# Binary cross entropy on one core: who negates, and in how many pieces

## The chip, the cores and the metric

The kernel runs on one core of one Trainium2 chip. A core has five engines that run side by side, each with its own list of instructions: TensorE (PE, not used here), VectorE (DVE), ScalarE (ACT), GpSimd (POOL) and SyncE (SP). Sixteen DMA engines move data between the large memory (HBM) and the core's on-chip memory of 128 partitions (SBUF). A transfer is issued by an instruction on POOL, ACT or SP, goes into that engine's queue, and the DMA engines work the queue off in order. The metric is device time in microseconds (us); less is better. The time before is 1867.55 us, the median of 3 runs (1865.96 to 1867.95).

## The reference

Two float32 arrays of 8192 x 8192, `pred` and `target` (zeros and ones), give one of the same shape:

```python
eps = 1e-7
pred = np.clip(pred, eps, 1 - eps)
return -(target * np.log(pred) + (1 - target) * np.log(1 - pred))
```

Because a target is 0 or 1, the kernel computes the same as -log(|(target - 1) + pred|) after the clip: for target 1 this is -log(pred), for target 0 it is -log(1 - pred).

## The kernel before

**Tiles.** The arrays are seen as one flat row of elements, which is cut into 39 chunks. A chunk of width w is 128 partitions by w columns. Chunk 0 has 8192 columns, chunks 1 to 35 have `WIDE` = 14336, and the last three (`TAIL`) have 6656, 6656 and 1024. In the code `z` is 35, the last wide chunk, and `a, b, c` are the three tail chunks.

**Buffers.** `ring_p` holds three slots of 14336 float32 columns. A chunk's pred values are loaded into its slot, worked on in place by all steps, and stored from there. Chunk k + 2 uses the slot of chunk k - 1, so its load has to wait for that chunk's store. `ring_t` has room for one chunk of targets, which the load casts from float32 to bfloat16, so the targets of chunk k + 1 can be loaded only when chunk k has been merged.

**Steps of a chunk**, each on all columns or on one half of them (`halves`):
- `clip` (VectorE, L85): max with 1e-7, then min with 1 - 1e-7, one instruction.
- `merge` (L91, L94, L95): VectorE forms (target - 1) + pred; ScalarE then takes the absolute value (Abs), and then the logarithm (Ln).
- `negate` (VectorE, L99): times -1.
- `load_p` (L70), `load_t` (L73), `store` (L79): transfers. All are issued on POOL, but for the first pred load (ACT's queue) and the stores of the three tail chunks (SP's queue).

**Order.** The order on each engine is written out by hand (`manual_schedule`): an engine runs its instructions as they stand in the source, and waits at each for the data it needs. One turn of the loop over chunks (L110 to L120) gives, for chunk k: both halves merged; the targets of k + 1 loaded; both halves negated; both halves of chunk k + 1 clipped; chunk k stored; the pred values of k + 2 loaded. On VectorE a turn is therefore merge, merge, negate, negate, clip, clip; on ScalarE Abs, Ln, Abs, Ln; on POOL the issue of a target load, of a store, and of a pred load. A store waits for the second negation of its chunk, and the issues behind it on POOL wait with it. VectorE's clips stand behind the second negation, which waits for ScalarE's second Ln.

Of the kernel before, what the change touches and what calls it, by code (L numbers as in the profile page):

```python
# [1 line left out]

# [4 lines left out]

EPS = 1e-7

WIDE = 14336  # L10
SLOTS = 3
TAIL = (6656, 6656, 1024)
ROWS = (108, 12, 8)


@with_exitstack
def kernel(
    ctx: ExitStack,
    tc: tile.TileContext,
    pred: bass.AP,  # L20
    target: bass.AP,
    out: bass.AP,
):
    nc = tc.nc
    fp32 = mybir.dt.float32
    low = mybir.dt.bfloat16
    Alu = mybir.AluOpType
    Act = mybir.ActivationFunctionType
    P = nc.NUM_PARTITIONS

    R, C = pred.shape
    total = R * C // P
    rest = total - sum(TAIL)
    n = rest // WIDE
    first = rest - n * WIDE
    assert 0 < first <= WIDE and n > 4 and sum(TAIL) <= WIDE
    spots = [(first, 0)]
    spots += [(WIDE, k % SLOTS * WIDE) for k in range(1, n + 1)]
    c = (n + 1) % SLOTS * WIDE
    for w in TAIL:  # L40
        spots.append((w, c))
        c += w
    n = len(spots)
    z = n - 1 - len(TAIL)
    starts = [sum(w for w, _ in spots[:k]) * P for k in range(n)]

    pool = ctx.enter_context(tc.tile_pool(name="rings", bufs=1))
    ring_p = pool.tile([P, SLOTS * WIDE], fp32, name="ring_p", tag="ring_p")
    ring_t = pool.tile([P, WIDE], low, name="ring_t", tag="ring_t")
    warm = pool.tile([1, 8], fp32, name="warm", tag="warm")  # L50

    def chunk(ap, k):
        flat = ap.rearrange("r c -> (r c)")
        w = spots[k][0]
        return flat[starts[k] : starts[k] + w * P].rearrange("(p w) -> p w", p=P)

    def cols(ring, k, part, c):
        w = spots[k][0]
        i, m = part
        return ring[:, c + i * w // m : c + (i + 1) * w // m]  # L60

    def p_of(k, part=(0, 1)):
        return cols(ring_p, k, part, spots[k][1])

    def t_of(k, part=(0, 1)):
        return cols(ring_t, k, part, spots[k][1] % WIDE)

    def load_p(k):
        queue = nc.scalar if k == 0 else nc.gpsimd
        queue.dma_start(out=p_of(k), in_=chunk(pred, k))  # L70

    def load_t(k):
        nc.gpsimd.dma_start(out=t_of(k), in_=chunk(target, k))  # L73

    def store(k):
        queue = nc.sync if k > z else nc.gpsimd
        r = 0
        for rows in ROWS if k == n - 1 else (P,):
            queue.dma_start(out=chunk(out, k)[r : r + rows, :], in_=p_of(k)[r : r + rows, :])  # L79
            r += rows  # L80
        assert r == P

    def clip(k, *part):
        p = p_of(k, *part)
        nc.vector.tensor_scalar(  # L85
            out=p, in0=p, scalar1=EPS, scalar2=1 - EPS, op0=Alu.max, op1=Alu.min
        )

    def merge(k, *part):
        p, t = p_of(k, *part), t_of(k, *part)  # L90
        nc.vector.scalar_tensor_tensor(  # L91
            out=p, in0=t, scalar=1.0, in1=p, op0=Alu.subtract, op1=Alu.add
        )
        nc.scalar.activation(out=p, in_=p, func=Act.Abs)  # L94
        nc.scalar.activation(out=p, in_=p, func=Act.Ln)  # L95

    def negate(k, *part):
        p = p_of(k, *part)
        nc.vector.tensor_scalar(out=p, in0=p, scalar1=-1.0, scalar2=None, op0=Alu.mult)  # L99

    halves = (0, 2), (1, 2)
    with tc.manual_schedule():
        load_p(0)
        load_t(0)
        load_p(1)
        nc.vector.memset(warm, 1.0)  # L106
        nc.scalar.activation(out=warm, in_=warm, func=Act.Ln)  # L107
        for h in halves:
            clip(0, h)
        for k in range(z):  # L110
            for h in halves:
                merge(k, h)
            load_t(k + 1)
            for h in halves:
                negate(k, h)
            for h in halves:
                clip(k + 1, h)
            store(k)
            if k + 2 <= z:
                load_p(k + 2)  # L120
        for h in halves:
            merge(z, h)
        a, b, c = range(z + 1, n)
        for j in a, b, c:
            load_p(j)
            load_t(j)
        negate(z, halves[0])
        clip(a)
        negate(z, halves[1])
        store(z)  # L130
        merge(a)
        clip(b)
        merge(b)
        negate(a)
        store(a)
        clip(c)
        merge(c)
        negate(b)
        store(b)
        negate(c)  # L140
        store(c)


# [1 line left out]
_INS = ['pred', 'target']  # L145
_OUTS = [((8192, 8192), 'float32')]


# [23 lines left out]
```

## Time and profile before

| what | value |
|---|---|
| median of 3 runs | 1867.55 us |
| profiled execution | 1868.84 us, span 1867.1 us |
| VectorE busy | 1118.2 us, 60% of the span |
| ScalarE busy | 901.7 us, 48% |
| POOL busy | 283.3 us, 15% |
| moved by DMA (as written to SBUF or HBM) | 671.14 MB, mean 359 GB/s |
| HBM read, written | 536.87 MB, 268.44 MB |
| L91, merge on VectorE, 7168 columns | 70 times, mean 7.62 us |
| L94 Abs and L95 Ln on ScalarE, 7168 columns | 70 times each, mean 6.17 and 6.18 us |
| L85 clip and L99 negation on VectorE, 7168 columns | 70 times each, mean 3.89 us |

How to read the profile. Times in it are us from the start of the span unless marked ns. A row of the timeline gives start, duration, engine, line of the source, operation, the buffer written and read, the shape, and how many like instructions in a row were merged into it (x2); in square brackets stands how long the engine sat idle before it and whose end it waited for. An issue on POOL is shown as DMA_DIRECT2D with the time that POOL spends on it. A slice row gives the span in 40 equal parts, the busy share of each as a digit in tenths (9 is 90% or more). The chain that ended last is followed back from the last instruction, at each step to what released it; "issue" is time in it for which the profile shows no wait. A window row gives, for a stretch of the span, the busy time of each engine with the number of instructions, the share of the DMA engines' time that was busy, and the GB/s moved; bytes and busy time of a DMA packet are booked where the packet starts, so in windows of 1 us or less shares over 1 and zeros alternate.

### The profile page before, as it was taken

The numbers are of one execution on the slowest core, as the hardware profiler recorded it, in microseconds if no ns is written. First come the engines' busy times: TensorE is split into PE (matmuls) and PEld (weight loads), VectorE is DVE, ScalarE is ACT, GpSimd is POOL, SyncE is SP. The second block draws the span as 40 slices with busy tenths as digits, with TensorE's granted clock in tenths as the row PEclk, the third lists the DMA queues.
The fourth block names the chain that finished last, engine by engine and source line by source line (L and its number), as shares of the span: only waits on it lengthen the run. The fifth ranks groups of instructions, "written<-read, shape, count | busy, mean of one in ns | idle before, by whom it ended". The sixth has DMA issues, their size and how long they took to land.

```text
span 1867.1 us, 695 instructions
## 1 busy us (share of the span) xinstructions
DVE 1118.2 (60%) x226; ACT 901.7 (48%) x152; POOL 283.3 (15%) x117
## 2 busy tenths in 40 slices
DVE  4675665655556555665665556655566665556664
ACT  3555444444555555444444555555544444455555
POOL 0121111111111101111111111101111111111100
DMA  9999999999999999999999999999999999999998
GB/s 331 336 373 373 364 355 359 356 355 355 354 354 359 373 373 373 370 356 362 356 354 358 354 354 356 367 373 373 373 362 360 359 354 359 354 354 354 360 366 346
DMA packets 16869, 671.14 MB, mean 359 GB/s; under 512 B 1888, under 2 KB 1888, under 8 KB 2272
## 3 DMA queue, kind: packets, MB, share of 16 engines
q0 software_dynamic: 16272, 659.56, 98.5%
q1 hardware_dynamic: 448, 7.34, 0.9%
q10 hardware_dynamic: 144, 4.19, 0.6%
q14 instruction: 5, 0.04, 0.0%
HBM read 536.87 MB, written 268.44 MB: 431 GB/s over the span
## 4 chain that ended last, share of the span: by engine, by line
DMA 67%; issue 28%; DVE 2%; ACT 2%; POOL 0%; POOLq 0%; DVEq 0%; PEldq 0%
DMA ring_t<-in_target_dram 67%; DVE ring_p L91 2%; ACT ring_p L95 1%; ACT ring_p L94 1%; DVE ring_p L99 0%; POOL out_dram L79 0%; POOL ring_p L70 0%; DVEq L167 0%; POOLq L73 0%; POOLq L79 0%; DVEq L91 0%; PEldq L167 0%
## 5 line engine op out<-in xcount | busy, mean ns | idle before, releaser
L94 ACT ACTIVATE ring_p<-ring_p 128x7168 f32<-128x7168 f32 (+3 forms) x75 | 451.6, 6021 | 943.5 <-DVE ring_p L91 943.5
L91 DVE SCALAR_TENSOR_TENSOR ring_p<-ring_t,ring_p 128x7168 f32<-128x7168 bf16 (+3 forms) x75 | 554.8, 7436 | 236.9 <-DMA ring_t<-in_target_dram 236.8
L99 DVE TENSOR_SCALAR ring_p<-ring_p 128x7168 f32<-128x7168 f32 (+3 forms) x75 | 285.0, 3801 | 475.0 <-ACT ring_p L95 475.0
L95 ACT ACTIVATE ring_p<-ring_p 128x7168 f32<-128x7168 f32 (+3 forms) x75 | 452.1, 6028 | 2.4
L85 DVE TENSOR_SCALAR ring_p<-ring_p 128x7168 f32<-128x7168 f32 (+3 forms) x75 | 281.8, 3798 | 20.1 <-DMA ring_p<-in_pred_dram 20.1
L79 POOL DMA_DIRECT2D out_dram<-ring_p x36 | 127.4, 3540 | 730.3 <-DVE ring_p L99 730.3
L73 POOL DMA_DIRECT2D ring_t<-in_target_dram x39 | 20.7, 532 | 802.9 <-DVE ring_p L91 802.1
L70 POOL DMA_DIRECT2D ring_p<-in_pred_dram x38 | 135.3, 3560 | 0.0
L107 ACT ACT_TABLE_LOAD x1 | 1.3, 1283 | 1.1 <-PEq L156 1.1
L106 DVE MEMSET warm<- 1x8 f32 x1 | 0.1, 65 | 0.8 <-PEq L156 0.8
L107 ACT ACTIVATE warm<-warm 1x8 f32<-1x8 f32 x1 | 0.2, 208 | 0.0
L156 POOL MEMSET const-float32-0.0<- 128x1 f32 x1 | 0.1, 98 | 0.2 <-issue 0.2
L156 POOL MEMSET const-bfloat16-1.0<- 128x1 bf16 x1 | 0.1, 101 | 0.0
L156 POOL MEMSET const-float32-1.0<- 128x1 f32 x1 | 0.1, 98 | 0.0
L156 POOL MEMSET const-uint8-127<- 128x1 uint8 x1 | 0.1, 98 | 0.0
## 6 DMA issues: line engine op xcount, KB each, us to landing
ring_p<-in_pred_dram POOLq DMA_DIRECT2D x35, 7168.0 KB, 44.3
out_dram<-ring_p POOLq DMA_DIRECT2D x35, 7168.0 KB, 31.0
ring_t<-in_target_dram POOLq DMA_DIRECT2D x35, 3584.0 KB, 35.2
ring_p<-in_pred_dram POOLq DMA_DIRECT2D x2, 3328.0 KB, 33.6
out_dram<-ring_p SPq DMA_DIRECT2D x2, 3328.0 KB, 15.1
ring_p<-in_pred_dram ACTq DMA_DIRECT2D x1, 4096.0 KB, 19.5
out_dram<-ring_p POOLq DMA_DIRECT2D x1, 4096.0 KB, 21.4
ring_t<-in_target_dram POOLq DMA_DIRECT2D x2, 1664.0 KB, 28.8
```

The costliest lines, as they stand in the source:

```text
L70: queue.dma_start(out=p_of(k), in_=chunk(pred, k))
L73: nc.gpsimd.dma_start(out=t_of(k), in_=chunk(target, k))
L79: queue.dma_start(out=chunk(out, k)[r : r + rows, :], in_=p_of(k)[r : r + rows, :])
L85: nc.vector.tensor_scalar(out=p, in0=p, scalar1=EPS, scalar2=1 - EPS, op0=Alu.max, op1=Alu.min)
L91: nc.vector.scalar_tensor_tensor(out=p, in0=t, scalar=1.0, in1=p, op0=Alu.subtract, op1=Alu.add)
L94: nc.scalar.activation(out=p, in_=p, func=Act.Abs)
L95: nc.scalar.activation(out=p, in_=p, func=Act.Ln)
L99: nc.vector.tensor_scalar(out=p, in0=p, scalar1=-1.0, scalar2=None, op0=Alu.mult)
L106: nc.vector.memset(warm, 1.0)
L107: nc.scalar.activation(out=warm, in_=warm, func=Act.Ln)
L156: nc = _bacc.Bacc("TRN2", target_bir_lowering=False, num_devices=1)
```

## The change

Logarithms leave `merge` and become a function of their own, `log`, so that both halves can be merged (VectorE and Abs) before one Ln instruction covers the whole chunk. A new function, `flip`, negates on ScalarE. Chunk 0 and all following chunks are clipped in one instruction. In the loop, chunk 0 takes one Ln and one negation on VectorE, chunk 1 keeps logarithms and VectorE's negations in halves, and chunks 2 to 34 take one Ln and one negation on ScalarE. Chunk 35 (`z`) and the three tail chunks keep the order they had.

```diff
@@ -92,7 +92,14 @@
             out=p, in0=t, scalar=1.0, in1=p, op0=Alu.subtract, op1=Alu.add
         )
         nc.scalar.activation(out=p, in_=p, func=Act.Abs)
+
+    def log(k, *part):
+        p = p_of(k, *part)
         nc.scalar.activation(out=p, in_=p, func=Act.Ln)
+
+    def flip(k, *part):
+        p = p_of(k, *part)
+        nc.scalar.mul(p, p, -1.0)
 
     def negate(k, *part):
         p = p_of(k, *part)
@@ -105,21 +112,26 @@
-        for h in halves:
-            clip(0, h)
+        clip(0)
         for k in range(z):
             for h in halves:
                 merge(k, h)
+                if k == 1:
+                    log(k, h)
             load_t(k + 1)
-            for h in halves:
-                negate(k, h)
-            for h in halves:
-                clip(k + 1, h)
+            if k == 1:
+                for h in halves:
+                    negate(k, h)
+            else:
+                log(k)
+                negate(k) if k == 0 else flip(k)
+            clip(k + 1)
             store(k)
             if k + 2 <= z:
                 load_p(k + 2)
         for h in halves:
             merge(z, h)
+            log(z, h)
...
         merge(a)
+        log(a)
         clip(b)
         merge(b)
+        log(b)
...
         merge(c)
+        log(c)
```

## The prediction

> **What bounds the kernel now.** I read the slices of the page first, then the chain that ended last, then the timeline of one chunk in the middle, and last the DMA columns of short windows around the places where one transfer follows another. The slices:
>
> ```profile
> DVE  4675665655556555665665556655566665556664
> ACT  3555444444555555444444555555544444455555
> POOL 0121111111111101111111111101111111111100
> DMA  9999999999999999999999999999999999999998
> ```
>
> No engine is near full, and the DMA engines are, in every slice; over 2 to 1850 us their share is 1.00. The chain says the same another way. Each chunk has one `ring_t` buffer, so the load of the next targets is issued after the merge and lands 35 us later, behind what is already queued:
>
> ```profile
> 168.07 35.69 DMA ring_t<-in_target_dram
> 203.81 15.50 issue
> 219.32 35.78 DMA ring_t<-in_target_dram
> ...
> 729.08 35.17 DMA ring_t<-in_target_dram
> 764.30 15.49 issue
> 779.81 35.19 DMA ring_t<-in_target_dram
> ```
>
> From one issue to the next is the period of a chunk: 51.25 us early, 50.73 us later, that is three transfers (store, pred, target) of 16.9 us. Only two things can change the time: the queue runs dry, or the transfers themselves get slower. So I ask when each transfer is on the queue and when it is needed. One chunk in the middle:
>
> ```profile
> 699.09 7.70 DVE L85 TENSOR_SCALAR ring_p<-ring_p 128x7168 f32<-128x7168 f32 x2
> 699.47 3.63 POOL L79 DMA_DIRECT2D out_dram<-ring_p  x1 [20.56 <-DVE ring_p L99]
> 703.09 3.82 POOL L70 DMA_DIRECT2D ring_p<-in_pred_dram  x1
> 713.63 15.16 DVE L91 SCALAR_TENSOR_TENSOR ring_p<-ring_t,ring_p 128x7168 f32<-128x7168 bf16 x2 [6.84 <-DMA ring_t<-in_target_dram]
> 729.08 0.53 POOL L73 DMA_DIRECT2D ring_t<-in_target_dram  x1 [22.18 <-DVE ring_p L91]
> 745.98 3.89 DVE L99 TENSOR_SCALAR ring_p<-ring_p 128x7168 f32<-128x7168 f32 x1 [8.38 <-ACT ring_p L95]
> 749.79 7.70 DVE L85 TENSOR_SCALAR ring_p<-ring_p 128x7168 f32<-128x7168 f32 x2
> 750.17 3.63 POOL L79 DMA_DIRECT2D out_dram<-ring_p  x1 [20.55 <-DVE ring_p L99]
> ```
>
> Call the start of a chunk's first merge M (713.63; the next is 764.35). The store is issued at M+36.5 and its issue ends at M+40.2. It is needed when the DMA engines finish the next target load. The 2 us windows show that moment, since a target load counts only its bf16 bytes: they read 229 GB/s to 708, 358 in 708 to 710 and 459 from 712. So the first engines pass from targets to the store at about M-5.6 and the last just before M, seen from the next chunk at M+45.1 to M+50.5. The store's descriptors are there 5 us before the first engine wants them.
>
> The last thing to see is POOL's issues. They take 3.63 and 3.82 us beside a clip and 0.53 us with no clip running (L73 above; the last store on POOL, at 1816.18 beside a merge, took 0.54). Each ends as one clip instruction ends: at chunk 1 the two halves run 93.76 to 101.46, and the issues end near 97.76 and 101.57.
>
> ```profile
> 93.76 7.70 DVE L85 TENSOR_SCALAR ring_p<-ring_p 128x7168 f32<-128x7168 f32 x2
> 94.14 3.62 POOL L79 DMA_DIRECT2D out_dram<-ring_p  x1 [20.56 <-DVE ring_p L99]
> 97.75 3.82 POOL L70 DMA_DIRECT2D ring_p<-in_pred_dram  x1
> ```
>
> **The change, chunks 2 to 34.** ScalarE's passes cost 6.18 us for 7168 columns and 3.62 for 4096: 0.833 ns a column and 0.21 fixed, so 12.15 for 14336. VectorE's clip costs 3.89 and 2.29: 0.521 ns and 0.16, so 7.63 whole. Merges are the same. The new chain from M: merges to 15.2, the second Abs to 21.4, the whole Ln to 33.6, the whole negation on ScalarE to 45.8, POOL's issue 0.30 later at 46.1. I price the negation like L94 and L95, which cost the same for two functions; below that only VectorE's 7.63 would be possible, above it a table load (L107, 1.28) ahead of each, which the changed program's list of instructions does not hold. VectorE loses 7.8 us of negation a chunk, worth nothing: it waits 6.84 us for targets already.
>
> The clip moves up. It has only its pred load to wait for (issued 703.09, 44.3 us to landing, so M+33.8) and runs to M+41.4; its cover until the next M grows from 6.9 to 9.3 us. At M+46.1 no clip runs, so the store's issue takes 0.53 and ends at M+46.6, 6.4 us later than now. From there to the first bytes the trace has no price on an idle queue. Above: chunk 1's store, issue ended 97.76, first bytes 100.0 to 100.6 right behind the targets, so 2.3 at most. Below: zero. Nearest: the first load on ScalarE's queue, issue ended 1.11, most first bytes 1.75 to 2.0, so 0.7, which I take. The store starts at M+47.3 (46.6 to 48.9). The first DMA engines wait 2.2 us for it, the last, which set when targets land, do not: 3.2 us of cover are left (1.6 at the worst). Cost: nothing. Without that cover each us late costs half a us per chunk, since store, pred and target then follow each other over two chunks.
>
> Behind the store on POOL stand the next pred load (needed 16.9 us later) and the next target load (issued at the next M+15.5 as before): nothing. Behind the negation on ScalarE stands the next Abs, at the next M+7.7, which is M+58.4: 12.6 us of cover. SP's queue is untouched, and the last chunks run the same instructions in the same order.
>
> **Chunks 0 and 1.** Here VectorE still negates, and the single clip holds POOL longer. Chunk 0: Abs of the second half ends at 37.0, whole Ln (7.03) 44.1, whole negation (4.42) 48.6. The store is issued at 48.9 in place of 46.11, meets a clip that runs 48.6 to 56.2, and ends at 56.35 in place of 49.73. First bytes at 57.05 with 0.7, where now they start at 56.5 to 57.2: a cost between 0 and 1.8, taken 0.2. Chunk 1: its chain is unchanged (logs and negations in halves), so the store meets the clip at 94.1 as now, but the clip is one instruction to 101.4. The issue ends at 101.5 and the bytes start at 102.2 in place of 100.3. Sum for the head: **1.9 us** (1.2 with no delay, 3.5 with 2.3), the 0.2 of chunk 0 being inside it.
>
> That takes POOL's issue as held to the end of the instruction. Read instead as a fixed 3.6 us beside any clip, it would end at 97.8 and the head would cost only chunk 0's share, nearly nothing; two issues ending on two clip halves speak for the first reading. The Trainium skill, SBUF — State Buffer (Who interferes with whom), calls it a lock on a shared port pair, held for the whole instruction in such passes of VectorE; the trace agrees, with issues that end 0.1 us after a clip instruction. The Trainium skill, DMA: Bandwidth & Descriptors (Specifications), gives about 1 us to the first byte on the GpSimd path against 0.6 on the other; by that the head would cost 2.2, an estimate.
>
> **Sum.** The profiled execution took 1868.84 (span 1867.1), 1.29 over the median of 1867.55. 1868.84 + 1.9 = 1870.7; against the median, **1869.5**. A tenth of a per cent is under what a measurement of this kernel tells from no change, about 0.2% (3.7 us).
>
> **The rivals.**
> (a) Slower: the queue runs dry in every chunk. If descriptors written by an idle POOL need more than 3.9 us from the issue's end to the first byte, even the last DMA engine waits (46.6 + d + 50.7 + 0.2 against two periods of 101.45). At 5 us that is 0.53 a chunk over 33 chunks, 17, and 6.2 at the head: 1891. For it: no row shows an idle queue fed by POOL. Against: the 2.3 bound.
> (b) Slower: the DMA engines are kept in step. A late store lets the early ones wait, so they all pass from targets to the store together. Early in the trace they do (starts within 150.5 to 152.5, against 709 to 714 later), and there the periods are 51.25, 51.32, 51.42, 51.59. Kept up over the 25 later chunks at 0.6 more each, 15 us with the head's 1.9: 1884. Against: at 100 us they passed in step with no lengthening, and there the store too had come just in time.
> (c) The lengthening goes altogether, for that same reason. The early periods exceed 50.73 by 3.5 us in all; less 1.9 at the head gives 1866.0, and 1865.2 at the least. With the DMA share at 1.00 there is hardly more to win.
>
> **How the numbers follow.** Forecast 62%, own range 1867 to 1873: same 46, slower 14, faster 2. (a) 10%, all slower. (b) 15%: slower 13, same 2. (c) 13%: same 7, faster 6. Together faster 0.08, same 0.55, slower 0.37. The range 1864.5 to 1881 takes in the forecast, nearly all of (c) and the weaker half of (b); it leaves out (a) and the rest.
>
> **What would show it.** DMA at 9 in all slices. POOL's L79 at 0.53 from chunk 2 on, and 7 us for the first two stores. The store of chunk 2 issued 46.1 after its merge starts, ScalarE busy about 1295 us in all (901.7 and 33 negations, less 33 fixed parts), VectorE about 856. The target load of chunk 3 issued at 116.8 as now, that of chunk 4 about 2 us later than 168.07, and periods near 50.7 in the long run. Wrong if the windows before M fall under a share of 1.00 for all engines (a), if the periods stay at 51.3 (b), or if ScalarE's negation takes well over 12.2 us.

## The result and the profile after

The changed kernel takes 1885.01 us (median, 1881.28 to 1886.68) against 1866.88 us: a ratio of 1.0094 with a 95% interval of 1.0077 to 1.0112. It is slower by 18 us. The forecast was 1869.5 and no change that can be told; the range ended at 1881.

The slices of the page of the changed kernel:

```profile
DVE  3753444444344444444444344443444443434464
ACT  3566666677777766666767677766666667777755
POOL 0210000000000000000000000000000000000000
DMA  9999999999999999999999999999999999999998
```

The engines' work moved as worked out: VectorE 861.5 us, ScalarE 1299.5, POOL 73.6. The DMA engines still look full in every slice. The busy share does not show the loss at all; the periods of the chunks do. The chain that ended last (start, us, what), first the head, then some chunks late in the span:

```profile
117.65 36.71 DMA ring_t<-in_target_dram
154.40 15.49 issue
169.91 35.45 DMA ring_t<-in_target_dram
...
1348.90 36.46 DMA ring_t<-in_target_dram
1385.40 15.49 issue
1400.91 35.24 DMA ring_t<-in_target_dram
1436.19 15.49 issue
1451.69 36.45 DMA ring_t<-in_target_dram
```

Chunk 4's targets are issued at 169.91 in place of 168.07: 1.84 us lost at the head. Later the periods alternate, 52.01 (1348.90 to 1400.91) and 50.78 (to 1451.69), where the kernel before has 50.7 to 50.8 in every chunk from 9 on but one (51.39). From chunk 9 to 34 the mean is 51.38 against 50.76. One chunk of that part (timeline; M is again the start of a chunk's first merge, here 1230.60):

```profile
1230.60 15.16 DVE L91 SCALAR_TENSOR_TENSOR ring_p<-ring_t,ring_p 128x7168 f32<-128x7168 bf16 x2 [9.37 <-DMA ring_t<-in_target_dram]
1264.18 12.15 ACT L102 ACTIVATE ring_p<-ring_p 128x14336 f32<-128x14336 f32 x1
1264.55 7.63 DVE L85 TENSOR_SCALAR ring_p<-ring_p 128x14336 f32<-128x14336 f32 x1 [18.79 <-DMA ring_p<-in_pred_dram]
1276.63 0.54 POOL L79 DMA_DIRECT2D out_dram<-ring_p  x1 [30.05 <-ACT ring_p L102]
1277.16 0.53 POOL L70 DMA_DIRECT2D ring_p<-in_pred_dram  x1
```

The store is issued at M+46.0, its issue takes 0.54, the clip ended at M+41.6, the negation costs 12.15. All of that is as forecast. What went wrong lies behind the issue, in the transfers.

The trace's single DMA packets tell more than its groups of instructions. A packet of a wide chunk takes 2.12 us, and each of the 16 DMA engines moves 8 of them per transfer. The DMA engines do not stay level: some finish a transfer some us before others, and are called the engines ahead here, the others the engines behind. In the kernel before, from chunk 12 on, two of 8,835 packets are longer by over 0.1 us. In the changed kernel, from chunk 14 on, the last packet of a store is longer, by about 0.4 and 0.8 us in turn, on the 13 engines that run ahead; on the 3 that run behind, the last target packets are longer (2.3 to 3.9 us in place of 2.13). From chunk 9 to 34 the DMA share is 1.00 in both kernels, so the time went into longer packets and not into idle engines.

When the 16 engines finish the targets, in us before the next merge starts (about chunk 32):

| kernel | engines ahead | engines behind |
|---|---|---|
| before | 11 between 5.2 and 4.0 | 3.0, 2.8, 2.4, 1.8, 0.4 |
| changed | 13 between 3.5 and 3.2 (chunk 33: 4.2 to 3.9) | 0.8, 0.6, 0.4 |
| changed, 3.6 us later still (run `later4` below) | all between 1.0 and 0.4 | none |

### The profile page after: what moved, and what is told of

Read it like the earlier page. It is cut to its first block, busy times and chain, and to the rows that moved or that the text cites. A ratio compares the mean times of both kernels' runs of the same rounds, so it can differ in the third digit from the quotient of the medians.

```text
span 1884.9 us, 584 instructions
## 1 busy us (share of the span) xinstructions
DVE 861.5 (46%) x123; ACT 1299.5 (69%) x151; POOL 73.6 (4%) x117
## 4 chain that ended last, share of the span: by engine, by line
DMA 68%; issue 27%; DVE 3%; ACT 1%; POOLq 0%; DVEq 0%
DMA ring_t<-in_target_dram 67%; DVE ring_p L91 2%; DMA ring_p<-in_pred_dram 1%; ACT ring_p L94 0%; ACT ring_p L98 0%; DVE ring_p L85 0%; DVE ring_p L106 0%; DVEq L182 0%; POOLq L73 0%; POOLq L79 0%; DVEq L91 0%
## 5 line engine op out<-in xcount | busy, mean ns | idle before, releaser
L94 ACT ACTIVATE ring_p<-ring_p 128x7168 f32<-128x7168 f32 (+3 forms) x75 | 452.1, 6028 | 563.6 <-DVE ring_p L91 563.6
L85 DVE TENSOR_SCALAR ring_p<-ring_p 128x14336 f32<-128x14336 f32 (+3 forms) x39 | 279.3, 7161 | 640.2 <-DMA ring_p<-in_pred_dram 640.2
L98 ACT ACTIVATE ring_p<-ring_p 128x14336 f32<-128x14336 f32 (+4 forms) x41 | 445.2, 10859 | 1.3
L102 ACT ACTIVATE ring_p<-ring_p 128x14336 f32<-128x14336 f32 x33 | 401.0, 12151 | 1.1
L79 POOL DMA_DIRECT2D out_dram<-ring_p x36 | 33.0, 916 | 1046.1 <-ACT ring_p L102 991.4
L106 DVE TENSOR_SCALAR ring_p<-ring_p 128x7168 f32<-128x7168 f32 (+3 forms) x8 | 27.9, 3492 | 39.1 <-ACT ring_p L98 39.1
L70 POOL DMA_DIRECT2D ring_p<-in_pred_dram x38 | 20.0, 527 | 0.0
## 6 DMA issues: line engine op xcount, KB each, us to landing
ring_p<-in_pred_dram POOLq DMA_DIRECT2D x35, 7168.0 KB, 38.3
out_dram<-ring_p POOLq DMA_DIRECT2D x35, 7168.0 KB, 22.2
out_dram<-ring_p SPq DMA_DIRECT2D x2, 3328.0 KB, 15.2
```

The source lines that it names most:

```text
L85: nc.vector.tensor_scalar(out=p, in0=p, scalar1=EPS, scalar2=1 - EPS, op0=Alu.max, op1=Alu.min)
L102: nc.scalar.mul(p, p, -1.0)
```

## The experiments

Theory L: the store's issue ends too close to the moment when the DMA engines need it. Theory S: the transfers are slowed by what runs beside them (ScalarE's long passes, DMA engines kept in step), whenever the store is issued.

**The store 1 us later.** A ScalarE pass of 1024 columns ahead of the negation:

```diff
     def flip(k, *part):
         p = p_of(k, *part)
+        nc.scalar.mul(p[:, 0:1024], p[:, 0:1024], 1.0)
         nc.scalar.mul(p, p, -1.0)
```

> A ScalarE pass of 1024 columns (1.06 us, times 1) stands ahead of each negation of chunks 2 to 34, so each store is issued 1.06 us later, at M+47.2 in place of M+46.1; nothing else moves. Theory L (the loss comes from the store's issue ending too close to the moment when the DMA engines need it): store, pred and target follow each other over two chunks, so half a us per chunk is lost for each us of delay, 33 x 0.53 = 17 us more, about 1902. Theory S (the transfers are slowed by what runs beside them, that is ScalarE's long passes or DMA engines kept in step, not by when the store is issued): no change, about 1885.

Measured 1890.59 (ratio 1.0113, 1.0090 to 1.0136), beside a before of 1866.99. The median grew by 5.6 us, neither 0 nor 17, and even that is not clear of noise: the intervals of the two kernels overlap, and one of the four runs took 1881.95. The trace says more. In chunks 3 to 7 all engines are in step (targets finished within 0.3 us of each other) and the periods are 50.67 to 50.85: no loss, with the store's issue 2.4 us ahead of the first engine that wants it. The loss comes from chunk 8 on, when the engines have spread.

**A quarter of the negation on VectorE**, so the store comes 3 us earlier:

```diff
-                negate(k) if k == 0 else flip(k)
+                if k == 0:
+                    negate(k)
+                else:
+                    negate(k, (0, 4))
+                    flip(k)
...
     def flip(k, *part):
-        p = p_of(k, *part)
+        p = p_of(k, *part)[:, spots[k][0] // 4 :]
         nc.scalar.mul(p, p, -1.0)
```

> VectorE negates the first quarter of the columns of chunks 2 to 34 ahead of the next clip, ScalarE the other three quarters. The store's issue ends near M+43.5 in place of M+46.6; whole logarithms and clips stay. Theory L: the store is again 3 us early, the loss per chunk goes, only the head's 1 to 2 us stay: 1867 to 1870. Theory S: ScalarE still works in long passes and the DMA engines are as much in step: 1880 to 1885.

Measured 1873.83 (1.0033, 1.0021 to 1.0045). Most of the loss goes, not all, and the time is above both numbers of theory L. In its profiled execution (1877.72) the store packets get longer in number only from chunk 27 on, when the engines ahead finish the targets 6.4 us before the next merge: M+44.8, 1.2 us after the store's issue ends. Chunks 26 to 34 take 51.27 us each. But chunks 9 to 25 take 50.92 with hardly a longer store packet: what is lost there, while the engines still spread, is not shown to come from the late store.

**ScalarE's negation alone**, in halves, in the kernel before:

```diff
         nc.scalar.activation(out=p, in_=p, func=Act.Ln)
+        if 2 <= k < z:
+            nc.scalar.mul(p, p, -1.0)
...
-            for h in halves:
-                negate(k, h)
+            if k < 2:
+                for h in halves:
+                    negate(k, h)
```

> The kernel before with one part of the change: ScalarE negates chunks 2 to 34, but in halves, right after each half's logarithm; clips, logarithms and the first chunks as before. The second half's negation ends near M+44.8, the store's issue near M+45.6: 1 us earlier than in the changed kernel, 5 us later than before. Theory L: the loss of 0.66 us a chunk falls by half a us, to 0.1 to 0.2: 1870 to 1873. Theory S, by ScalarE's negation: 1883 to 1885; by the passes being whole instead of halved: 1867.

Measured 1879.56 (1.0066, 1.0049 to 1.0083): between the two theories' numbers. The linear slope that I had put into theory L was wrong; this run alone decides nothing.

**The pred load ahead of the store** on POOL, in the changed kernel:

```diff
-            store(k)
             if k + 2 <= z:
                 load_p(k + 2)
+            store(k)
```

> The changed kernel with the order of two issues on POOL swapped in the loop: the pred load of chunk k+2 ahead of the store of chunk k. The negation on ScalarE and the time of the store's issue stay (M+46), but the store now stands behind a pred load that is issued once the store before has landed, so the DMA engines need it about 17 us later. Theory L: the loss goes, 1866 to 1870. Theory S: the same passes and the same step of the DMA engines, 1880 to 1885.

Measured 1872.05 (1.0028, 1.0018 to 1.0037). The store is issued as late as in the changed kernel (M+46), but 13 of the 18 us are gone. That speaks for L, though the time is above its 1870. Chunk 3 is merged at 151.94 here (152.62 in the kernel before), so the rest is not the head. Chunks 9 to 34 take 51.05 us each: the last packet of the pred load is longer on some engines, most often on those behind, while those ahead run on to 8.9 us ahead.

**VectorE late, ScalarE as before.** The clip moves ahead of the second negation in the kernel before; no ScalarE instruction changes:

```diff
-            for h in halves:
-                negate(k, h)
+            negate(k, halves[0])
+            if k < 2:
+                negate(k, halves[1])
             for h in halves:
                 clip(k + 1, h)
+            if k >= 2:
+                negate(k, halves[1])
```

> The kernel before, but from chunk 2 on VectorE clips the next chunk ahead of the second negation. ScalarE's work stays as before, no pass is whole, nothing is negated on ScalarE; only the store is late: clips to M+41.5, negation to M+45.4, POOL's issue ended at M+46.2 (changed kernel: M+46.6, before: M+40.2). Theory L (lateness of the store alone): the changed kernel's loss of chunks 3 to 34, 15 us, comes back: 1880 to 1883. Theory S (ScalarE's longer work beside the transfers): 1867.

Measured 1882.27 (1.0077, 1.0062 to 1.0092), beside a before of 1867.61. One chunk of it:

```profile
1230.51 15.16 DVE L91 SCALAR_TENSOR_TENSOR ring_p<-ring_t,ring_p 128x7168 f32<-128x7168 bf16 x2 [6.07 <-DMA ring_t<-in_target_dram]
1264.24 7.70 DVE L85 TENSOR_SCALAR ring_p<-ring_p 128x7168 f32<-128x7168 f32 x2 [9.76 <-DMA ring_p<-in_pred_dram]
1271.85 3.89 DVE L99 TENSOR_SCALAR ring_p<-ring_p 128x7168 f32<-128x7168 f32 x1
1276.03 0.54 POOL L79 DMA_DIRECT2D out_dram<-ring_p  x1 [29.54 <-DVE ring_p L99]
```

The store's issue ends at M+46.1 for another reason, and the changed kernel's loss is back, 14.7 us, with the same alternation (mean periods 51.76 and 50.96). This shows that a late store is enough for the loss, with ScalarE's work as before. The pred load behind the store is late by as much here, as in the changed kernel, but it is needed only a transfer later.

**ScalarE busy, store on time.** The kernel before with work for ScalarE on a buffer of its own (128 x 2816):

```diff
+            if k >= 2:
+                for i in range(5):
+                    nc.scalar.mul(spare, spare, 1.0)
```

> The kernel before with five ScalarE passes of 2816 columns (2.6 us each, 12.8 in all, about what the negation takes) on a buffer of their own after each chunk's second logarithm, from chunk 2 on. The store's time stays at M+36.5 to M+40.2. Theory L: 1867. Theory S: 1875 to 1885.

Measured 1868.25 (1.0003, 0.9993 to 1.0012). ScalarE works on after the second logarithm, and the store is issued at M+36.5 as before (line numbers are one higher in this kernel, and the view ends at 752):

```profile
714.02 15.16 DVE L92 SCALAR_TENSOR_TENSOR ring_p<-ring_t,ring_p 128x7168 f32<-128x7168 bf16 x2 [7.25 <-DMA ring_t<-in_target_dram]
746.24 7.70 ACT L118 ACTIVATE spare<-spare 128x2816 f32<-128x2816 f32 x3
750.56 3.63 POOL L80 DMA_DIRECT2D out_dram<-ring_p  x1 [20.55 <-DVE ring_p L100]
```

Theory S falls as far as ScalarE's work goes.

**The swap in the kernel before:**

> The kernel before with the same swap on POOL as in the run with the changed kernel (pred load ahead of the store in the loop), nothing else. That run kept 5 us over the kernel before, 2 of them from the head, 3 unexplained. If they come from the swap itself (other order of transfers, an end without a pred load to fill the queue): 1869 to 1872. If they come from ScalarE's work: 1867 or less.

Measured 1870.59 (1.0015, 1.0006 to 1.0024): 3 us. So most of what the swap left over in the changed kernel comes with the swap itself.

**The head undone.** Chunks 0 and 1 clipped, logged and negated in halves as before, the rest as changed:

> The changed kernel with chunks 0 and 1 clipped, logged and negated in halves as before; the rest is the changed kernel. The head's part of the prediction says 1.9 us less, so 1883, with chunk 3 merged at 152.6 in place of 154.45. If the head also sets how the DMA engines stand to each other later on, the loss of the later chunks changes too: anywhere from 1878 to 1888.

Measured 1882.24 (1.0076, 1.0061 to 1.0091): 2.8 us less than the changed kernel, within the bounds of 1.2 to 3.5, but the intervals of the two overlap. Chunk 3 is merged at 151.89, earlier than the 152.6 expected.

**How late is too late.** Two more points, 3.6 us later than the changed kernel (the pass of the first experiment with 4096 columns) and 2 us later than the kernel before:

```diff
         nc.scalar.activation(out=p, in_=p, func=Act.Abs)
+        if 2 <= k < z and part[0] == halves[1]:
+            nc.scalar.mul(p[:, 0:2200], p[:, 0:2200], 1.0)
```

> As the run with 1024 columns more, but with 4096: 3.62 us later, the store's issue ends near M+50.2, when all but the last DMA engines have long finished the targets. So far each us of delay cost about 0.2 us a chunk, not the 0.5 of two chunks following each other. If it stays at 0.2: 24 us over the changed kernel, 1909. If from here on all engines wait and the two-chunk arithmetic holds, with the 5 us from the issue's end to the working store that the changed kernel's periods would mean: (50.2 + 5 + 50.9) / 2 = 53.05 a chunk, 1941.

> The kernel before with a ScalarE pass of 2200 columns (2.0 us, times 1) on the second half of chunks 2 to 34, ahead of its logarithm: the store is issued at M+38.5 and its issue ends at M+42.2, 2 us later than before and 1.3 us earlier than in the run with a quarter of the negation on VectorE. If the cost grows evenly from the kernel before on (12.6 us at 5.4 us later, 15 at 6.0): about 5, 1872. If it starts only where the early engines have to wait: 1867 to 1869.

`later4` measured 1896.65 (1.0156, 1.0141 to 1.0172), `mild` 1868.33 (1.0009, 0.9998 to 1.0019). Being 2 us later costs nothing that can be told, as the second of the two cases for it said; beyond that it costs. `later4` lies under both of its numbers, 1909 and 1941. In `later4` the periods alternate from chunk 3 on, and all 16 engines stay in step:

```profile
892.28 36.24 DMA ring_t<-in_target_dram
928.57 15.49 issue
944.08 35.94 DMA ring_t<-in_target_dram
980.06 15.49 issue
995.57 36.26 DMA ring_t<-in_target_dram
```

Two periods are 103.29 (892.28 to 995.57). Store, pred and target after each other make 50.7 of that, landing and the wait for the merge about 0.2, and the store's issue ends at M+50.2: 103.3 - 50.2 - 50.9 leaves 2.2 us between the end of the issue and what a store at full speed would need. Where these 2.2 us stand is seen in windows of half a us (us, then VectorE, ScalarE, POOL, clock, DMA share, GB/s). All 16 engines start a packet together, every 2.1 us:

```profile
978.50:979.00 0.50, 0.00 (x0) 0.00 (x0) 0.50 (x2) 1.00 0.00 0
979.00:979.50 0.50, 0.00 (x0) 0.00 (x0) 0.35 (x1) 1.00 2.25 918
979.50:980.00 0.50, 0.00 (x0) 0.00 (x0) 0.00 (x0) 1.00 2.17 918
...
992.00:992.50 0.50, 0.50 (x1) 0.50 (x1) 0.00 (x0) 1.00 4.24 1835
...
994.00:994.50 0.50, 0.50 (x1) 0.00 (x0) 0.00 (x0) 1.00 5.78 1835
```

A packet's time is booked where it starts, so a share of 4.24 in half a us is 2.12 us per engine. Packet by packet, the engines finish the targets between 979.16 and 979.67, and the store's first packets start between 979.40 and 979.65, 0.56 to 0.81 us after its issue ended at 978.84: no engine stands still for more than about 0.25 us. These first packets take up to 2.25 us and the next six are normal, the last of them at 992; the eighth and last of the store, at 994, has a share of 5.78: 2.89 us. Of the 2.2 us, 0.6 to 0.8 pass before the first packets, and 0.77 are paid at the far end of the store, ahead of the next pred load; the rest was not taken apart.

**Stores on another queue.** All stores on SP's queue, in both kernels (`queue = nc.sync` in `store`):

> The kernel before with all stores issued on SP's queue instead of POOL's. They are then not held by a clip, and a store no longer stands in one queue behind the targets: the DMA engines take packets of both queues. The pred load on POOL waits for its slot alone. If the 3.5 us of long periods of chunks 2 to 9 come from targets and store following each other in one queue: 1863 to 1865. If two queues only change who waits: 1867; worse if the targets, which the next merge waits for, are slowed by the store: 1870 to 1890.

> The changed kernel with all stores on SP's queue. The next pred load is on POOL's queue as soon as the store before has landed, near M+17, so when an engine has finished the targets it has a pred load to go on with and the store's time matters no more. Theory L: the loss goes, 1865 to 1870. Theory S: 1880 to 1885.

Measured 1925.34 (1.0317, 1.0284 to 1.0350) and 1951.20 (1.0476, 1.0397 to 1.0556). Both forecasts missed, by 35 us and more: I had expected the second to be free of the loss. The DMA issues of `spafter` (KB each, us from issue to landing) show what two queues do:

```profile
ring_p<-in_pred_dram POOLq DMA_DIRECT2D x35, 7168.0 KB, 53.0
out_dram<-ring_p SPq DMA_DIRECT2D x35, 7168.0 KB, 39.0
```

In the changed kernel these took 38.3 and 22.2. The next pred load waits on POOL until the store before has landed, and both now take longer; in some chunks the queues do run dry (three slices of its page at 303, 291 and 278 GB/s, with a DMA share of 0.87 to 0.89). How much of the loss comes from each was not taken apart.

The points put together. "Needed" is when the first DMA engine finishes the targets and wants the store, from the same M, as the median of the last ten wide chunks. The periods are the mean of chunks 9 to 34. Both are of the profiled execution.

| run | store's issue ends, M+ | needed, M+ | period | over the kernel before |
|---|---|---|---|---|
| before | 40.2 | 45.5 | 50.76 | - |
| `filler` | 40.2 | 45.6 | 50.79 | 0.6 |
| `mild` | 42.2 | 46.5 | 50.78 | 1.3 |
| `split` | 43.6 | 44.5 | 51.04 | 6.8, head included |
| `fliponly` | 45.6 | 46.3 | 51.24 | 12.6 |
| `veclate` | 46.1 | 46.9 | 51.36 | 14.7 |
| `headback` | 46.6 | 47.5 | 51.27 | 14.6 |
| changed | 46.6 | 47.5 | 51.38 | 18.1, head included |
| `later` | 47.7 | 48.2 | 51.60 | 23.6, head included |
| `later4` | 50.2 | 50.7 | 51.65 | 29.6, head included |
| `swap` | 46.6 | a transfer later | 51.05 | 5.1 |

In the kernels that lose about half a us a chunk or more, the end of the issue is at last less than 1 us ahead of the first engine that wants the store; in those that lose next to nothing (before, `filler`, `mild`), 4 us or more are left. `split` comes down to 1 us only in its last chunks. `swapbefore`, `spbefore` and `spafter`, which change the order or the queue, are not in the table. No version was faster than the kernel before by more than its runs scatter.

## Why the prediction was wrong, point by point

**The bound and the two ways to lose time** were read rightly: queue dry, or transfers slower. The changed kernel stands between them: behind the head the DMA share stays at 1.00, and yet packets get longer when the store comes late.

**The prices** held: 12.15 for the negation (L102, 12.151 mean), 0.54 for POOL's issue with no clip running, the store at M+46.0 (46.1 forecast), ScalarE 1299.5 us (1295), VectorE 861.5 (856).

**The head's** total held, 1.9 forecast and 1.84 in the profile, but its terms did not, and that they add up is luck. Chunk 0's store started when forecast (56.98 to 57.13), after the engines had stood idle for about 1 us, but its last packet took 1.7 to 2.3 us in place of 1.21, so the next store began 1.2 us later than in the kernel before, and not 0.2. Chunk 1's store started right behind the targets, at 101.28 to 101.74 and not at 102.2, and cost the other 0.6 us at its own last packet (2.77 us in place of 2.17, means of the 16 engines). What held is the reading of the lock, as the two issues beside the whole clips show:

```profile
48.67 7.62 DVE L85 TENSOR_SCALAR ring_p<-ring_p 128x14336 f32<-128x14336 f32 x1
49.05 7.36 POOL L79 DMA_DIRECT2D out_dram<-ring_p  x1 [14.64 <-DVE ring_p L106]
...
93.20 7.36 POOL L79 DMA_DIRECT2D out_dram<-ring_p  x1 [20.55 <-DVE ring_p L106]
```

POOL is held to the end of the clip, 7.36 us, not for a fixed 3.6. The Trainium skill, SBUF — State Buffer (Who interferes with whom), which calls it a lock for the whole instruction, agrees.

**The step that failed** is the one for chunks 2 to 34: "The first DMA engines wait 2.2 us for it, the last, which set when targets land, do not ... Cost: nothing." It costs about half a us a chunk: of 17.1 us at chunk 35's merge (1796.71 against 1779.64), 15.2 came after the head. Two things in the step were wrong.
- The delay behind the issue was taken as 0.7 us, from the first load on another queue. As the time to the first bytes that was about right: 0.57 us behind chunk 0's store of the changed kernel (56.41 to 56.98), 0.56 in `later4`. But the step let the store run at full speed from there, and it does not: its last packet gets longer, by 0.77 us in `later4`, and in all `later4` has 2.2 us between the end of the issue and a store at full speed, nearly the upper bound of 2.3. By it the store of the changed kernel is ready at M+48.8 for engines that want it at M+47.2 to M+48.0 (periods of 50.8 and 52.2, less 3.6 and 4.2).
- I treated the engines ahead as a cushion that may shrink for free. It is not free. In the kernel before the spread grows over chunks 2 to 9, at a price of 3.5 us in long periods, until the engines ahead are 4.6 us early, and then nearly nothing is lost any more. In the changed kernel the late store holds the engines ahead at 3.2 to 4.2 us, and those behind go on losing as much on their last target packets. That holding them back keeps the loss going is read from the traces; no run sets the spread by itself. I had seen the early long periods, and had not asked what ended them.

**Rival (a)**, the queue dry for all engines, did not come: the first bytes follow 0.6 us behind the issue, and even with 2.2 us the last engine, needed at M+50.5, still had 1.7 us of cover. In `later4` all engines want the store within 2.2 us of its issue; those 2.2 us are worked out with (a)'s two-chunk sum, so the run is no test of that sum. **Rival (b)** gave 1884, near the measured time, and half of its reason came true: the early engines are held back (3.5 to 4.2 us ahead, against 5.2), and the periods stay 0.6 us longer, which is the sign that was named for (b). The other half fell: the engines are not in step (3 us apart), and engines in step cost nothing by themselves (chunks 3 to 7 of `later`; `later4`, where no target packet is longer). **Rival (c)** did not come: chunks 3 to 8 average 51.07.

**Still open:** why the engines behind get longer target packets while the others already store, why that nearly stopped after chunk 11 in the kernel before and not in `swap` or `split`, and why a late store is paid at its end. A last packet can be long without a late transfer, too: in the kernel before, chunk 1's last target packets took 2.8 to 3.3 us with the store long on the queue, in the changed kernel 2.13 with nothing behind them. No run here separates these. One thing more goes with lateness: every kernel that loses half a us a chunk issues its store with no clip running (0.54 us), while the kernel before, `filler` and `mild` issue it beside one (3.6). Against this as the cause stand chunks 3 to 7 of `later`, issued in 0.54 us and without loss; no run keeps the time of the store and changes this alone.

## What to carry to other kernels

A kernel bound by DMA with its transfers in one queue needs each transfer issued well before the engines get to it, counted from the engines that run ahead, not from the one that lands last: here 4 us of margin at the end of the issue cost nothing (`mild`), nor did 2.4 us in the early chunks of `later`, and less than 1 us cost about half a us a chunk or more. The busy share stays full when that margin is gone; the period from chunk to chunk shows it. Moving work to an engine with free time can be a loss when it lengthens the chain to an issue with little time to spare, however idle the engine was.

## What the runs showed of the hardware that was not expected

- A transfer that comes late leaves little gap or none (at most 0.25 us in `later4`, about 1 us at chunk 0 of the changed kernel), but its own last packet is longer (2.89 in place of 2.12 us in `later4`).
- The 16 DMA engines, with equal work in one queue, drift up to 5 us apart in the kernel before and 9 in `swap`.
- Stores on a second queue made both kernels slower, by 3.2% and 4.8% over the kernel before.
